# Mixture-of-experts block: eight slots of 32 tokens in four 32-column tiles, a new order of slots, and alternating heads in the scan's products

## The chip, the cores and the metric

The kernel runs on one core of a Trainium2 chip. The metric is the device time of one execution in microseconds (us), from the core's first to its last instruction with what the launch adds. The core's engines are called as in the profile: PE (TensorE, with PEld for its weight loads), DVE (VectorE), ACT (ScalarE), POOL (GpSimd) and SP (the queue from which most loads are issued).

## What is computed

Two blocks follow each other on 512 tokens of width 1024. The first mixes a bidirectional state-space scan (32 heads of 64, 4 groups, chunks of 128 tokens) with a Fourier branch, and then sends each token through 4 of 32 experts. The second has attention, a gated recurrence and a dense feed-forward part. The change touches the scan and the experts of the first block:

```python
# scan, per chunk (forward, and backward on the reversed sequence); the two directions are added
cb = jnp.einsum('bclgn,bcsgn->bcgls', cc, bc)
y_diag = jnp.einsum('bcgls,bcghls,bcsghp->bclghp', cb, decay_in, xdt)
y_off = jnp.einsum('bclgn,bcghpn,bclgh->bclghp', cc, h_prev, jnp.exp(a_cs))

# experts: 512 tokens x 4 choices = 2048 rows over 32 experts
logits = (tok @ w_router + b_router).astype(jnp.float32)
top_logit, top_idx = lax.top_k(logits, TOP_K)
top_w = jax.nn.softmax(top_logit, axis=-1)
gu = xe @ w_gate_up[e] + b_gate_up[e]              # 1024 -> 2048, for the rows of expert e
gate = jnp.minimum(gu[:, :D_FF], SWIGLU_LIMIT)
up = jnp.clip(gu[:, D_FF:], -SWIGLU_LIMIT, SWIGLU_LIMIT)
act = (up + 1.0) * gate * jax.nn.sigmoid(SWIGLU_ALPHA * gate)
y = act @ w_down[e] + b_down[e]                    # 1024 -> 1024, times the row's weight, added to its token
```

All weights are float32. One expert's are 8 MB (up) and 4 MB (down), so 32 experts read 384 MB.

## The kernel before

**The scan.** `mixer` walks over 16 pairs of heads (`p`). For each pair PE projects the next pair's inputs (`px`, `pc`, three reduced-precision products for one of float32, lines 99 to 101), builds the states (`pst`), and then does the diagonal part `py` (line 669) and the part from the states `po` (line 677). `py` is one PSUM bank of 128 partitions: head `j` = 0 takes partitions 0 to 63, head 1 takes 64 to 127, and four token blocks `b` and two directions `d` are accumulated into each. The loops run over `j`, then `d`, then `b`, so that four products in a row, and then four more, go to the same half of the partitions. These products are full float32; in the trace one of them is two PE instructions.

**The experts.** `moe` handles 32 slots in the order of `ORDER`. Slots 0 and 1 are experts 0 and 1, so that their weights can be loaded before the router has finished; the other slots hold the other experts by the number of their tokens, the smallest first. A slot has a width, which is the number of tokens that it has room for:

- slots 0 to 15 (`HALF`) are half slots, of 64 tokens. The 64 tokens are the stationary operand of a 128x64 product, and two such products, with different columns of the weights, run into the lower and the upper 64 partitions of PSUM (`half_mm`, line 1262). These are float32 products straight from the loaded weights (`wraw`).
- slots 16 to 29 are full slots, of 128 tokens. Here the weights are split by ACT (`whi`, line 86) and DVE (`wlo`, line 87) into two reduced-precision parts, and three products (lines 99 to 101) do the work of one.
- slots 30 and 31 (`DOUBLE`) are a full and a half block with the same weights.

Experts with more tokens than their slot has room for get further passes of a loop at the end (`For_i`), as often as the router's counts need; on these inputs the loop runs zero times.

In turn `t` PE does the up products of slot `t` (tile `pgh` of a half slot, `pg` of a full one) and the down products of the slot before (`pd`, or `pdh` beside a full block). Tokens are gathered by an indirect DMA (`h_scr` to `xg`), transposed on PE (`pt`), and the result is scaled on ACT, multiplied by `g2b` on POOL (line 1336) and added to its rows in DRAM by an indirect DMA (`x_scr`). Half slots gather and scatter half rows of 2 KB.

Weights come in pieces of 1 MB, eight for up and four for down of each slot, all issued from SP in the order of use, into a ring of 13 buffers (`W.rings`). A piece is loaded as soon as the buffer 13 pieces earlier has been used up. The instruction order on each engine is fixed at build time by a scheduler.

The lines that pick the width and the order are:

```python
HALF = range(0, 16)
DOUBLE = (30, 31)
ORDER = (0, 1, 16, 17, 2, 3, 18, 19, 4, 20, 5, 21, 6, 30, 7, 8, 22, 9, 23, 10, 24, 11, 31, 12, 13, 25, 26, 14, 27, 28,
         29, 15)
```

Of the kernel before, what the change touches and what calls it, by code (L numbers as in the profile page):

```python
# [8 lines left out]
F32 = mybir.dt.float32  # L9
F32R = mybir.dt.float32r  # L10
BF16 = mybir.dt.bfloat16
I32 = mybir.dt.int32
# [6 lines left out]
P = 128  # L19
D = 1024  # L20
# [84 lines left out]
TILE_WAITS = ('moeio', 'moeio3', 'ps_g', 'ps_mt', 'ps_d', 'outr', 'outp', 'mx', 'biasp', 'rows', 'b2io', 'b2t', 'b2r', 'res2', 'moeT', 'wraw3', 'wraw4')  # L105


class Kernel:
# [91 lines left out]
    def mixer(self):  # L200
# [391 lines left out]
        for p in range(16):  # L592
# [22 lines left out]
            for j in range(2):  # L615
                for d in range(2):
# [269 lines left out]
    def router(self, mx, keep, xT, ahead, st, stp):  # L886
# [59 lines left out]
        def choose(b, x1, rs, fill=lambda: None):  # L946
# [23 lines left out]
            self.chosen = nc.vector.tensor_scalar(pick[:, b, :], iota[:, 0:64], r[:, 0:1], None, op0=ALU.is_equal).ins  # L970

        def picked(b):

            for k in range(KD):
                nc.tensor.matmul(pts[0][:, k % 4, 64 * (k // 4):64 * (k // 4) + 64], h2s[b][0][:, k * P:(k + 1) * P],
# [13 lines left out]
        pick = xT[:, 0:256].rearrange("p (b l) -> p b l", l=64)  # L989
# [17 lines left out]
        xT4 = xT[:, 512:].rearrange("p (k t) -> p k t", k=4)  # L1007
        nc.scalar.copy(xT4[:, 0:2, :], pts[0][:, 0:2, :])
        nc.vector.tensor_copy(xT4[:, 2:4, :], pts[0][:, 2:4, :])
        ahead()  # L1010

        with self.behind((self.chosen,)):
            p0 = psl.tile([P, 1, 3], F32, tag='ptab', name='ptab0')
            self.table(rot, p0[:, 0, :], rm[:, :, 1:2], V[:, :, 1, 0:3], True, True)
            first = self.slots(keep, p0, 1, 'f', (0,))[0]
# [53 lines left out]
    def table(self, pool, out, place, v, first, half=False):  # L1069
# [3 lines left out]
        v4 = lambda x: x.rearrange("p b (h l) -> p b h l", h=2)  # L1073
        if half:
            nc.vector.tensor_tensor(v4(pe), self.rc[:, 0, None, None, 0:64].to_broadcast([P, NT, 2, 64]),
                                    place[:, :, :, None].to_broadcast([P, NT, 2, 64]), op=ALU.is_equal)
# [16 lines left out]
    def overflow(self, tp, psl, selb, ubf, obf, keep):  # L1093
# [3 lines left out]
        nc, cf = self.nc, self.rc  # L1097
# [10 lines left out]
        val = tp.tile([P, 2, 16], BF16, name='val')  # L1108
        for i, c in enumerate((16, 40)):
            nc.vector.tensor_scalar(val[:, i, :], cf[:, 2, 24:40], pos, cf[:, 2, c:c + 1], op0=ALU.is_equal, op1=ALU.mult)  # L1110
        nc.tensor.matmul(pc[:, 8:40], obf, val.rearrange("p i q -> p (i q)"), start=True, stop=True,
                         skip_group_check=True)
        nc.tensor.matmul(pc[:, 40:41], obf, fl, start=True, stop=True, skip_group_check=True)
        self.ext = ext = keep.tile([P, 33], F32, name='ext')
        nc.vector.tensor_copy(ext, pc[:, 8:41])

        no = tp.tile([P, 16], F32, name='noblk')
        nc.vector.tensor_scalar(no, ext[:, 16:32], 0.0, 4096.0, op0=ALU.is_equal, op1=ALU.mult)
        nc.vector.tensor_add(ext[:, 16:32], ext[:, 16:32], no)
        self.exti = keep.tile([P, 33], I32, name='exti')  # L1120
# [23 lines left out]
    def slots(self, pool, tab, n, sfx, halves=()):  # L1144


        nc = self.nc
        t = pool.tile([P, n, tab.shape[2]], F32, name='slott' + sfx)
# [6 lines left out]
        for j in halves:  # L1155
            nc.vector.tensor_scalar(f[:, 0, j:j + 1], f[:, 0, j:j + 1], 2.0, self.rc[:, 2, 41:42], op0=ALU.mult, op1=ALU.add)
# [7 lines left out]
    HALF = range(0, 16)  # L1164
# [830 lines left out]
```

## Time and profile before

| what | value |
|---|---|
| time, median of 3 runs | 2924.7 us (2928.36, 2915.26, 2924.7) |
| time of the profiled execution | 2918.13 us |
| its span, first to last instruction | 2916.3 us |
| PE busy | 2772.1 us, 95% |
| mean granted TensorE clock | 0.984 |
| DMA, mean over the span | 221 GB/s |
| scan of the first block | about 130 to 800 us |
| experts | about 950 to 2080 us |

Busy time of PE counts an instruction from its start to a modelled end, so neighbouring instructions overlap, and the step from one start to the next is the better price of one. A DMA share is the mean busy share of the core's 16 DMA engines; it can come out a little above 1. The profiled execution is 6.6 us faster than the median.

### The profile page before, as it was taken

How to read it: one execution, taken by the hardware profiler on the slowest of the kernel's cores; microseconds unless marked ns; L12 is line 12 of the kernel's file. 1: busy time of each engine (PE TensorE's matmuls, PEld its weight loads, DVE VectorE, ACT ScalarE, POOL GpSimd, SP SyncE). 2: the span in 40 equal slices, each digit the busy share in tenths (PEclk: the TensorE clock that was granted, in tenths of full speed). 3: DMA queues.
4: the chain of work that ended last, by engine and by line, in shares of the span. 5: the costliest groups of instructions: out<-in, count | busy, mean ns of one | idle time of the engine just before them, and what ended most of it. 6: DMA issues, size and time to landing. Idle time of an engine off the chain costs nothing. (4 is left out here: it accounts for less than half of the span.)

```text
span 2916.3 us, 37264 instructions
## 1 busy us (share of the span) xinstructions
PE 2772.1 (95%) x14084; PEld 2033.2 (70%) x14084; DVE 1773.7 (61%) x2557; ACT 1321.1 (45%) x1899; POOL 403.5 (14%) x388
## 2 busy tenths in 40 slices
PE   5999999999999999999999999999599999999999
PEld 3888878788887455555455554657288888788887
DVE  4637878787677565766445552768477777733322
ACT  4534545454444244544334442556356666632221
POOL 1211121212202111111111112120300000100000
PEclk9999999999999899999999999999799999999999
DMA  8243374744566899999699979998532132533321
GB/s 229 80 137 96 113 220 134 228 126 138 179 188 246 343 387 401 359 391 400 258 402 408 389 293 386 399 382 342 147 101 83 55 87 73 188 97 91 101 94 65
DMA packets 294839, 644.40 MB, mean 221 GB/s; under 512 B 18706, under 2 KB 190370, under 8 KB 258848
## 3 DMA queue, kind: packets, MB, share of 16 engines
q1 hardware_dynamic: 267552, 569.77, 53.3%
q0 software_dynamic: 25120, 67.93, 8.6%
q10 hardware_dynamic: 1984, 4.28, 0.4%
q8 instruction: 112, 1.84, 0.3%
q14 instruction: 71, 0.58, 0.1%
HBM read 617.54 MB, written 33.64 MB: 223 GB/s over the span
## 5 line engine op out<-in xcount | busy, mean ns | idle before, releaser
L87 DVE TENSOR_TENSOR wlo<-wraw,whi 128x1024 fp32r<-128x1024 f32 (+1 forms) x635 | 787.8, 1264 | 462.1 <-ACT whi L86 451.5
L86 ACT CAST whi<-wraw 128x1024 fp32r<-128x1024 f32 (+1 forms) x635 | 652.5, 1043 | 605.5 <-PE pf L100 153.2
L1262 PE MATMUL pgh<-wraw,xg 128*64 128x512 f32 x1152 | 279.7, 605 | 0.7 <-ACT xg L1241 0.7
L99 PE MATMUL px<-hThi,whi 128*128 128x512 f32 x576 | 229.9, 400 | 0.0
L101 PE MATMUL px<-hThi,wlo 128*128 128x512 f32 x576 | 225.9, 392 | 2.1 <-DVE wlo L87 2.1
L100 PE MATMUL px<-hTlo,whi 128*128 128x512 f32 x576 | 226.4, 393 | 0.0
L1262 PEld LDWEIGHTS pgh<-wraw,xg 128*64 128x64 f32 x1152 | 81.8, 138 | 154.0 <-issue 147.6
L1336 POOL TENSOR_TENSOR y<-y,g2b 64x512 f32<-64x512 f32 (+1 forms) x50 | 86.1, 1723 | 522.2 <-ACT y L1331 497.4
L100 PE MATMUL pg<-wlo,T0h 128*128 128x512 f32 x352 | 144.2, 410 | 5.5 <-DVE wlo L87 5.4
L100 PE MATMUL pf<-hnlo,whi 128*128 128x512 f32 (+1 forms) x384 | 142.4, 372 | 0.0
L101 PE MATMUL pf<-hnhi,wlo 128*128 128x512 f32 (+1 forms) x384 | 142.4, 372 | 0.0
L99 PE MATMUL pf<-hnhi,whi 128*128 128x512 f32 (+1 forms) x384 | 141.6, 372 | 0.0
L101 PE MATMUL pg<-whi,T0l 128*128 128x512 f32 x352 | 140.4, 399 | 0.0
L99 PE MATMUL pg<-whi,T0h 128*128 128x512 f32 x352 | 132.4, 405 | 3.4 <-ACT whi L86 3.4
L484 DVE SCALAR_TENSOR_TENSOR cacc<-cr,vecs,cacc 128x770 f32<-128x770 f32 (+1 forms) x128 | 121.7, 961 | 19.8 <-ACT cacc L482 18.7
L101 PEld LDWEIGHTS px<-hThi,wlo 128*128 128x128 f32 x576 | 108.3, 188 | 27.6 <-DVE wlo L87 2.9
L1262 PE MATMUL pd<-wraw,act 128*64 128x512 f32 x512 | 122.7, 599 | 0.0
L100 PEld LDWEIGHTS px<-hTlo,whi 128*128 128x128 f32 x576 | 109.0, 189 | 16.0 <-issue 1.7
L99 PEld LDWEIGHTS px<-hThi,whi 128*128 128x128 f32 x576 | 109.0, 189 | 15.7 <-issue 1.7
L1267 DVE TENSOR_SCALAR g<-pgh 128x512 f32<-128x512 f32 x18 | 12.4, 691 | 170.4 <-PE pgh L1262 170.3
L1268 ACT ACTIVATE g<-g 128x512 f32<-128x512 f32 (+1 forms) x34 | 28.2, 831 | 178.9 <-DVE g L1267 178.9
L623 ACT ACTIVATE m<-m,acs_tok 128x128 f32<-128x128 f32 x256 | 81.6, 390 | 58.3 <-DMA m<-acs_scr 56.6
(614 smaller groups left out, 6102.3 us busy)
## 6 DMA issues: line engine op xcount, KB each, us to landing
wraw<-in_w_gate_up SPq DMA_DIRECT2D x256, 1024.0 KB, 9.7
wraw<-in_w_down SPq DMA_DIRECT2D x128, 1024.0 KB, 9.9
wraw<-in_w_in SPq DMA_DIRECT2D x81, 512.0 KB, 6.6
wraw<-in_w_mod SPq DMA_DIRECT2D x23, 1024.0 KB, 9.1
wraw<-in_w_ffn_in SPq DMA_DIRECT2D x44, 512.0 KB, 5.2
wraw<-in_w_in SPq DMA_DIRECT2D x18, 1024.0 KB, 5.4
m<-acs_scr POOLq DMA_DIRECT2D x64, 256.0 KB, 5.3
wraw<-in_w_ffn_out SPq DMA_DIRECT2D x10, 1024.0 KB, 5.0
```

Source lines behind the costliest of these rows:

```text
L86: a = (copy or nc.scalar.copy)(dst[0], src)
L87: return a.ins, (eng or nc.vector).tensor_sub(dst[1], src, dst[0].bitcast(F32)).ins
L99: nc.tensor.matmul(out, a[0], b[0], start=first, stop=False)
L100: nc.tensor.matmul(out, a[0], b[1], start=False, stop=False)
L101: return nc.tensor.matmul(out, a[1], b[0], start=False, stop=last).ins
L484: nc.vector.scalar_tensor_tensor(acc, t[:, j:j + n], cw[:, j, ch:ch + 1], acc, op0=ALU.mult, op1=ALU.add)
L623: nc.scalar.activation(m[:, b, :], m[:, b, :], AF.Relu, bias=acs_tok[:, b, row:row + 1], scale=-1.0)
L1262: nc.tensor.matmul(out[64 * h:64 * h + 64], a, w, start=False, stop=last, skip_group_check=True)
L1267: nc.vector.tensor_scalar_min(g, gate, 7.0)
L1268: nc.scalar.activation(g, g, AF.Silu, scale=1.702)
L1336: nc.gpsimd.tensor_mul(y[q], y[q], g2b[q, c])
```

## The change

Three edits are made together.

1. **Quarter slots.** Slots 0 to 7 get a width of 32 tokens. Four products of 128x32, each with another part of the weights' columns, go to the four 32-partition parts of PSUM (`part_mm`). The tokens of such a slot are gathered and scattered as quarter rows of 1 KB. An up piece is still four products of 512 columns; a down piece is now eight products of 256 columns where a half slot has four of 512. `HALF` and `DOUBLE` become the table `WIDTHS`, the helpers take a width in place of a flag, the limits for the closing loop follow the widths, and that loop can hold 24 passes in place of 16.
2. **A new `ORDER`** of the slots.
3. **The scan's `py` products** run over `d`, then `b`, then `j`: consecutive products go to the two heads in turn. The tables `m` are made in the order of that use.

Besides, the pool of four rows of 1024 (`moeio3`) becomes three of these, and four rows of 512 (`moeio4`, tile `low`) for half and quarter slots.

```diff
-            for j in range(2):
-                for d in range(2):
+            for d in range(2):
+                for j in range(2):
                     row = 32 * d + h0 + j
                     m = pr4.tile([P, NT, P], F32, tag='m', name='m')
...
-            for j in range(2):
-                for d in range(2):
-                    for b in range(NT):
-                        nc.tensor.matmul(py[j * HD:(j + 1) * HD, b, :], xd[d][:, b, j, :], ms[2 * j + d][:, b, :],
+            for d in range(2):
+                for b in range(NT):
+                    for j in range(2):
+                        nc.tensor.matmul(py[j * HD:(j + 1) * HD, b, :], xd[d][:, b, j, :], ms[2 * d + j][:, b, :],
...
-    HALF = range(0, 16)
-    DOUBLE = (30, 31)
-    ORDER = (0, 1, 16, 17, 2, 3, 18, 19, 4, 20, 5, 21, 6, 30, 7, 8, 22, 9, 23, 10, 24, 11, 31, 12, 13, 25, 26, 14, 27, 28,
-             29, 15)
+    WIDTHS = ((8, (32,)), (16, (64,)), (30, (128,)), (32, (128, 64)))
+    ORDER = (0, 1, 16, 17, 8, 18, 9, 10, 19, 30, 2, 11, 20, 12, 21, 13, 22, 14, 3, 23, 24, 25, 4, 26, 27, 28, 5,
+             15, 29, 31, 6, 7)
+
+    NX = 24
...
-        io3 = self.pool('moeio3', 4, None, st)
+        io3 = self.pool('moeio3', 3, None, st)
+        io4 = self.pool('moeio4', 4, None, st)
...
-            nc.gpsimd.indirect_dma_start(out=x[:, :D // 2] if half else x, out_offset=None,
-                                         in_=halfrows(self.h2_d) if half else self.h2_d,
+            nc.gpsimd.indirect_dma_start(out=x[:, :D * w // P], out_offset=None, in_=rows(self.h2_d, w),
                                          in_offset=bass.IndirectOffsetOnAxis(ap=tok, axis=0),
...
-        def half_mm(out, xT, k, ws, last):
-            a = xT[:, k % 4, 64 * (k // 4):64 * (k // 4) + 64]
-            for h, w in enumerate(ws):
-                nc.tensor.matmul(out[64 * h:64 * h + 64], a, w, start=False, stop=last, skip_group_check=True)
+        def columns(w, x):
+
+            n = P // w
+            v = x.rearrange("p (g q c) -> p g q c", q=n, c=D // n)
+            return [v[:, :, q, :] for q in range(n)]
...
+        def part_mm(w, out, xT, k, ws, last):
+
+            n = KD * w // P
+            a = xT[:, k % n, k // n * w:k // n * w + w]
+            for i, o in enumerate(out):
+                for q, wq in enumerate(columns(w, ws)):
+                    m = wq.shape[1] // len(out)
+                    nc.tensor.matmul(o[w * q:w * q + w], a, wq[:, m * i:m * i + m, :], start=False, stop=last,
+                                     skip_group_check=True)
...
-                for q, c in qs:
+                for i in range(P // w):
+                    q, c = slice(w * i, w * i + w), slice(n * i, n * i + n)
                     if tail:
                         nc.vector.scalar_tensor_tensor(y[q], pd[q], wgt[q], g2b[q, c], op0=ALU.mult, op1=ALU.mult)
                     else:
                         nc.gpsimd.tensor_mul(y[q], y[q], g2b[q, c])
```

The scheduler decides where the new products stand, so three places of PE's order are shown. First the scan, one pair of heads. The numbers behind `m` and `xd` are buffers: `m_1920` and `m_1928` belong before to the two directions of head 0, and after to the two heads of the forward direction. Before:

```order
L101 MATMUL px_2048<-hThi_82,wlo_1899 128x512
L669 MATMUL py_2076<-m_1920,xd_1902 64x128 x4
L669 MATMUL py_2076<-m_1928,xd_1903 64x128 x4
L669 MATMUL py_2076<-m_1936,xd_1902 64x128 x4
L669 MATMUL py_2076<-m_1944,xd_1903 64x128 x4
L677 MATMUL po_2093<-C0_1785,Hn_2028 128x128
L677 MATMUL po_2093<-C0_1785,Hn_2033 128x128
```

After, the middle of the 16 products, where the direction changes:

```order
L669 MATMUL py_2076<-m_1920,xd_1902 64x128
L669 MATMUL py_2076<-m_1928,xd_1902 64x128
L669 MATMUL py_2076<-m_1920,xd_1902 64x128
L669 MATMUL py_2076<-m_1928,xd_1902 64x128
L669 MATMUL py_2076<-m_1936,xd_1903 64x128
L669 MATMUL py_2076<-m_1944,xd_1903 64x128
L669 MATMUL py_2076<-m_1936,xd_1903 64x128
L669 MATMUL py_2076<-m_1944,xd_1903 64x128
L669 MATMUL py_2076<-m_1936,xd_1903 64x128
```

Sixteen products are sixteen products; four in a row with one table become pairs that change the table, and with it the half of the partitions, at each step.

Second, the start of the experts, slot 0 (`xg_7499` are its tokens, `sel` and `bh` its bias, `pperm` and `povf` the end of the router). Before:

```order
L1254 LDWEIGHTS sel_7532
L1254 MATMUL pgh<-bh,sel_7532 64x512
L1254 LDWEIGHTS sel_7532
L1254 MATMUL pgh<-bh,sel_7532 64x512
L1262 MATMUL pgh<-wraw,xg_7499 64x512 x11
L1038 LDWEIGHTS eb
L1038 MATMUL pperm<-esel,eb 1x32
L1262 MATMUL pgh<-wraw,xg_7499 64x512 x2
L1101 LDWEIGHTS selb
```

After:

```order
L1277 LDWEIGHTS sel_7532
L1277 MATMUL pgh<-bh,sel_7532 32x512
L1277 LDWEIGHTS sel_7532
L1277 MATMUL pgh<-bh,sel_7532 32x512
L1288 MATMUL pgh<-wraw,xg_7499 32x512 x15
L1041 LDWEIGHTS eb
L1041 MATMUL pperm<-esel,eb 1x32
L1288 MATMUL pgh<-wraw,xg_7499 32x512 x3
L1105 LDWEIGHTS selb
```

The products keep their number and their 512 columns, and write 32 partitions in place of 64; the router's last products stand between them at a slightly later place.

Third, the turn behind double slot 30: the down products of the slot before it (`pd`), between the first up products of the slot behind it (`pgh`). Before, slot 6 (half) stands ahead and slot 7 (half) behind:

```order
L1262 MATMUL pd_11530<-wraw_11533,act_11048 64x512 x4
L1262 MATMUL pd_11530<-wraw_11539,act_11048 64x512 x4
L1262 MATMUL pd_11530<-wraw_11551,act_11048 64x512 x4
L1262 MATMUL pd_11530<-wraw_11557,act_11048 64x512 x4
L1262 MATMUL pgh_11584<-wraw_11623,xg1_7500 64x512 x4
L1262 MATMUL pgh_11584<-wraw_11629,xg1_7500 64x512 x4
L1262 MATMUL pgh_11584<-wraw_11635,xg1_7500 64x512 x4
```

After, slot 19 (full) stands ahead and slot 2 (quarter) behind:

```order
L1288 MATMUL pgh_10644<-wraw_10661,xg1_7500 32x512 x4
L1288 MATMUL pgh_10644<-wraw_10684,xg1_7500 32x512 x4
L1252 MATMUL pt_10702<-ident_66,row_10264 128x128 x8
L1272 LDWEIGHTS esel_8111
L1272 MATMUL pd_10528<-bh_6817,esel_8111 128x512
L1272 LDWEIGHTS esel_8111
L1272 MATMUL pd_10528<-bh_6817,esel_8111 128x512
L99 MATMUL pd_10528<-whi_10533,T0h_8231 128x512
L100 MATMUL pd_10528<-wlo_10534,T0h_8231 128x512
L101 MATMUL pd_10528<-whi_10533,T0l_8232 128x512
```

What is done in the double's wake is now a quarter's up and a full slot's down, where it was a half's up and a half's down.

## Rows read from the trace of the kernel before

**Rows 1.** the page, its head and busy times by engine (share of the span, instructions)
```profile
span 2916.3 us, 37264 instructions
...
PE 2772.1 (95%) x14084; PEld 2033.2 (70%) x14084; DVE 1773.7 (61%) x2557; ACT 1321.1 (45%) x1899; POOL 403.5 (14%) x388
```

**Rows 2.** windows: length, busy us of PE, PEld, DVE, ACT, POOL; clock, DMA share, GB/s
```profile
930.00:2050.00 1120.00, 1072.76 (x4845) 615.92 (x4846) 649.96 (x758) 492.75 (x517) 187.19 (x117) 0.98 0.95 370
1450.00:1690.00 240.00, 227.44 (x1007) 124.43 (x1006) 120.65 (x113) 99.55 (x107) 46.03 (x30) 0.99 1.01 400
1110.00:1370.00 260.00, 244.43 (x1137) 144.07 (x1134) 159.51 (x203) 118.86 (x124) 49.56 (x30) 0.99 0.99 388
130.00:760.00 630.00, 627.25 (x3755) 533.92 (x3754) 455.42 (x762) 303.65 (x608) 115.06 (x197) 1.00 0.48 144
```

**Rows 3.** windows of 40 us in the experts' stage, same columns
```profile
1370.00:1410.00 40.00, 40.00 (x162) 23.21 (x163) 26.43 (x31) 20.28 (x21) 4.62 (x2) 0.96 0.75 283
1410.00:1450.00 40.00, 40.00 (x183) 16.91 (x179) 12.94 (x12) 9.03 (x10) 4.11 (x3) 1.00 0.69 259
...
1690.00:1730.00 40.00, 40.00 (x159) 22.97 (x158) 23.01 (x19) 20.56 (x21) 6.32 (x3) 1.00 0.83 312
1730.00:1770.00 40.00, 40.00 (x180) 16.46 (x180) 11.46 (x11) 8.57 (x12) 2.54 (x2) 1.00 0.69 270
...
1970.00:2010.00 40.00, 37.57 (x164) 28.53 (x163) 34.97 (x30) 28.86 (x30) 5.00 (x2) 1.00 0.87 335
```

**Rows 4.** timeline of the SP queue: start, length of the group, loads
```profile
1469.69 18.37 SPq L61 DMA_DIRECT2D wraw<-in_w_gate_up  x8
...
1696.64 41.38 SPq L61 DMA_DIRECT2D wraw<-in_w_gate_up  x8
```

**Rows 5.** groups by line: count, busy us, mean ns, idle before
```profile
L1262 PE MATMUL pgh<-wraw,xg 128*64 128x512 f32 x1152 | 279.7, 605 | 0.7 <-ACT xg L1241 0.7
...
L1262 PE MATMUL pd<-wraw,act 128*64 128x512 f32 x512 | 122.7, 599 | 0.0
...
L1254 PE MATMUL pg<-bh,esel 96*128 96x512 bf16 x64 | 19.3, 383 | 9.7 <-DVE act L1269 9.7
...
L1245 PE MATMUL pt<-ident,act 128*128 128x128 f32 x128 | 17.4, 278 | 1.7 <-DVE act L1270 0.9 <-DVE slott L1149 0.8
L1245 PE MATMUL pt<-ident,xg 128*128 128x128 f32 x128 | 17.4, 277 | 1.5 <-DVE T1l L93 1.5
...
L515 PE MATMUL pm<-wraw,sc 128*32 128x512 f32 x128 | 16.2, 601 | 0.3 <-DMA wraw<-in_w_mod 0.3
```

**Rows 6.** timeline of PE inside a full slot: start, us, instruction
```profile
1049.90 0.40 PE L100 MATMUL pg<-wlo,T1h 128*128 128x512 f32 x1
...
1051.54 0.39 PE L100 MATMUL pg<-wlo,T1h 128*128 128x512 f32 x1
```

**Rows 7.** windows of 5 us at the start of the experts' stage
```profile
950.00:955.00 5.00, 3.98 (x18) 1.97 (x19) 5.00 (x19) 0.37 (x1) 0.00 (x0) 0.50 0.54 221
955.00:960.00 5.00, 5.00 (x21) 1.73 (x19) 1.50 (x4) 0.00 (x0) 1.11 (x1) 0.86 0.55 187
```

**Rows 8.** windows of 5 us at the end of the experts' stage
```profile
2055.00:2060.00 5.00, 3.68 (x17) 2.88 (x18) 4.75 (x5) 5.00 (x6) 0.00 (x0) 1.00 0.31 100
...
2075.00:2080.00 5.00, 1.96 (x10) 0.50 (x6) 1.50 (x2) 0.00 (x0) 0.87 (x1) 0.94 0.81 183
```

**Rows 9.** DMA queues from 955 to 963 us: packets, MB, share
```profile
q0 software_dynamic: 80, 0.09, 3.4%
```

**Rows 10.** groups by line: the scan's products
```profile
L669 PE MATMUL py<-m,xd 128*64 128x128 f32 x512 | 53.7, 276 | 0.0
```

**Rows 11.** timeline of PE in the scan, one pair of heads
```profile
258.99 3.33 PE L669 MATMUL py<-m,xd 128*64 128x128 f32 x32
262.25 2.05 PE L677 MATMUL po<-C,Hn 128*128 128x128 f32 x16
```

**Rows 12.** timeline of PE in the router
```profile
937.71 1.98 PE L975 MATMUL pt<-xg,h 128*128 128x64 f32 x16
```

More of the change, by code (lines that the diff above doesn't have):

```diff
@@ L1067, in router, with table @@
         return first
-    def table(self, pool, out, place, v, first, half=False):
+    def table(self, pool, out, place, v, first, w=P):
         nc = self.nc
         pe = pool.tile([P, NT, P], BF16, tag='pe', name='pe')
[L1073 to L1076, printed above, removed]
+        n = P // w
+        if n > 1:
+            nc.vector.tensor_tensor(pe.rearrange("p b (h l) -> p b h l", h=n),
+                                    self.rc[:, 0, None, None, 0:w].to_broadcast([P, NT, n, w]),
+                                    place[:, :, :, None].to_broadcast([P, NT, n, w]), op=ALU.is_equal)
         else:
@@ L1142, in extra, with slots @@
         return r[:, 0, :, None], v
-    def slots(self, pool, tab, n, sfx, halves=()):
-        nc = self.nc
-        t = pool.tile([P, n, tab.shape[2]], F32, name='slott' + sfx)
+    def slots(self, pool, tab, sfx, widths, tmp=None):
+        nc, n = self.nc, len(widths)
+        t = (tmp or pool).tile([P, n, tab.shape[2]], F32, name='slott' + ('' if tmp else sfx))
         nc.vector.tensor_copy(t, tab)
@@ new lines, in bias @@
+        def bias(w, out, selT, c, n):
+            b = bh[:, c:c + D * n]
+            if w == P:
+                for i, o in enumerate(out):
+                    nc.tensor.matmul(o, selT.to_broadcast([96, P]), b[:, 512 * i:512 * i + 512], start=True, stop=False)
+                return
+            for q, bq in enumerate(columns(w, b)):
+                for i, o in enumerate(out):
+                    g = n // len(out)
+                    nc.tensor.matmul(o[w * q:w * q + w], selT.to_broadcast([96, w]), bq[:, g * i:g * i + g, :],
+                                     start=True, stop=False, skip_group_check=True)
@@ L1359, in moe @@
         for s_ in self.ORDER:
-            blocks += [(s_, 0, s_ in self.HALF)] + ([(s_, P, True)] if s_ in self.DOUBLE else [])
+            ws = self.widths(s_)
+            blocks += [(s_, sum(ws[:i]), w) for i, w in enumerate(ws)]
         at = lambda e: [i for i, b in enumerate(blocks) if b[0] == e]
@@ L1369, in step @@
                 if j < n:
-                    e, o, half = blocks[i0 + j]
+                    e, o, w = blocks[i0 + j]
                     src = self.rm[:, :, e:e + 1]
@@ L1389, in moe @@
             nx = at(self.ORDER[turn + 1]) if turn < NE - 1 else []
+            assert not (nx and len(xTs) == 2 and xTs[0][0] < P and blocks[nx[0]][2] == P)
             if e < 2:
@@ L1951, in layout @@
     rc[:, 0, :] = l
[L1952 removed]
+    rc[:, 2, 41], rc[:, 2, 42] = l // 64, l // 32
     rc[:, 1, :] = l[:, None] < l
```

185 lines of the change are left out of this document (94 added, 91 removed).

## The prediction

> **What bounds the kernel now.** I began with the page's busy times [rows 1]: TensorE (PE) is busy for 2772.1 of 2916.3 us, so work taken off it can shorten the run, but only where no other engine ends last. That is asked stage by stage, with the windows view [rows 2]. In the scan's stage (130 to 760 us) PE is busy for 627.25 of 630 us and the DMA engines for 48%: PE alone is the bound, and a microsecond saved there is a microsecond of the run. In the experts' stage (930 to 2050 us) two things are nearly full at once: PE 1072.76 of 1120 us, DMA share 0.95. So 0.05 x 1120 = 56 us is all that the loads could still give there, however little PE has to do.
>
> Where do the loads pause? The 40 us windows [rows 3] show it: shares of 0.75 and 0.69 from 1370 us, 0.83 and 0.69 from 1690 us, which is 22.4 and 19.2 us of idle DMA, while PE stands at 40.00. These are the places of the two double slots (30 and 31): PE falls behind, the 13 pieces of buffer fill, the loads wait. A smaller one is at 1970 us (0.87, 5.2 us), in the run of full slots at the end. The SP queue's timeline gives the pace of the loads in between [rows 4]: seven slots from 1469.69 to 1696.64 us, 32.4 us a slot.
>
> **What a slot costs PE.** Half slot: two alternating column halves take 279.7 / 1152 = 0.243 us an instruction of 512 columns (one float32 product is two) [rows 5]. 18 half blocks have 64 such up and 32 down (122.7 / 512 = 0.240): 15.5 + 7.7 = 23.2, with about 2 us of biases and transposes 25. Full slot: 144 products at the step seen from 1049.90 to 1051.54 us, seven products later [rows 6], 0.234 us: 33.7; transposes and biases (17.4 + 17.4 + 19.3) / 16 = 3.4 [rows 5]; together 37. Double: 62. A quarter slot is not in the trace, but four 32-column tiles with four different streams are: `pm` at L515, 16.2 / 128 = 0.127 us an instruction [rows 5]. Up is again 64 of 512 columns, 8.1 us; down is 64 of 256 columns, between half of that (4.1) and the same (8.1), I take 5. With half the transposes, 14.5. So each of eight slots loses about 10.5 us, 84 us of PE in all (bounds 60 and 95).
>
> **What of the 84 us shows.** Against 32.4 us of loads, a full slot puts PE 4.6 us behind, a double 30, a half lets it gain 7.4, a quarter 18; it can't get ahead of the loads, so the lag stops at zero. Before, both doubles begin at a lag near 0 and reach 30; the pauses of 22 and 19 say that the ring covers about 10. In the new order each double stands behind a full slot (19, 30 and 29, 31): 35 at its end, 25 us of pause by this count. But behind it now comes a quarter, which empties the ring at about 1 us a piece (8 x 0.127) where a half takes 1.9 (8 x 0.243), and part of the pause lies in that following slot (the windows at 1410 and 1730 us). I take 0 for the doubles, bounds -10 and +10. The runs of three full slots (23 to 25, 26 to 28) reach 14, 4 over the cover, twice; that answers to the 5.2 at the end before: 0, bounds -8 and +4. The rest of the idle 56 us is thin (0.99 from 1110 us [rows 2]): -3.
>
> The start: from 950 to 960 us the share is 0.54 and 0.55 [rows 7], 4.5 us of pause, because slot 0's pieces hold the ring while PE works on them at half pace. Quarters free them in half the time: -4 (0 to -5).
>
> The end: the last weights land at about 2056.5 us (share 0.31 of 5 us from 2055), and PE ends at 2077 (1.96 us busy from 2075) [rows 8]: 20 us, in which slot 29's and 15's down products are caught up. With slots 6 and 7 last, PE gains 18 on each and is left with a down piece of 1 to 2 us and the closing chain, so I take -15 (-8 to -18). The first weights of the next block that are loaded in this shadow still lie beside the last scatter.
>
> Gathers and scatters: the first eight slots hold 178 tokens (counted by the reference's own router on its inputs: 25, 23, 16, 17, 18, 24, 25, 30). Rows of 1 KB instead of 2 make 356 more packets each way. In 955 to 963 us slot 1's gather is 80 packets, 0.09 MB, 3.4% of 8 us on 16 engines, 4.4 us of engine time for 46 rows [rows 9], 0.095 each: at that price 712 more cost 4.2 us of all 16 engines, at no price nothing; +2. POOL's two multiplications become four half as long, on an engine that is busy for 14% [rows 1]: nothing, and if they showed it would be behind the last slot only, whose product is DVE's. Smaller swiglu, tables and copies on DVE and ACT lie beside the loads. A second ring of four low rows and three full rows takes the place of four: a full slot's result waits for a scatter one slot old, which is some 30 us; nothing.
>
> Experts' stage: 0 + 0 - 3 - 4 - 15 + 2 = -20 (the bounds add up to -44 and +10).
>
> **The scan's products.** `py`: 512 instructions, 53.7 us [rows 10]; 32 a pair of heads, from 258.99 us to the next product at 262.25, 0.102 each [rows 11]. Four in a row went to one column half; now the halves alternate. Nearest row: the alternating halves of L1262, 0.243 for 512 columns, where one half at a time at py's rate would be 4 x 0.102 = 0.41; the same ratio makes 53.7 into 32, -22. But the streams are four times shorter, and weights may set the pace: with 128 weight columns and only 64 streamed, L975 goes no faster than (1.98 - 0.28) / 15 = 0.113 [rows 12], so 64 weight columns about 0.057, 512 x 0.057 = 29, -25. Adding L1262's excess over a plain halving (0.243 - 0.204 = 0.04 an instruction) to 0.051 gives 0.09, 46.6, -7. I take -18; bounds 0 and -26 (a perfect halving). PE has nothing else to wait for in this stage, so it passes to the run whole.
> A rule of the Trainium skill speaks against it: TensorE: Matmul & The Clock Gate, "Part 3: Packing small matmuls — row/col tiling", says that a weight load runs beside a product in flight only where the two differ in their row group, and here both heads use all 128 rows. By that rule py gains nothing, and the sum is -20 instead of -38. The trace leans the other way: L1262's two halves share all rows as well and run at 0.243, not 0.41.
>
> **Sum.** -20 - 18 = -38 on the profiled execution's 2918.1 us: 2880. That execution lies 6.6 us below the median of 2924.7 and 3.5 below the mean of the four times; 2880 + 3 gives **2883 us**. A measurement of this kernel tells about 0.5% (15 us) from no change.
>
> **Rivals.**
> *Only the scan gains.* If the count of lags holds (25 us at each double, 4 at each run of three) the +18 eat the end's -15 and the start: 2921.6 - 18 = 2904. For it: the loads are at 1.01 wherever PE isn't behind [rows 2]; against: the quarter right behind each double.
> *Only the experts' stage gains*: the weights of one head's half are not loaded before the other's stream is through, and py takes its 53.7 us as now [rows 10]: 2921.6 - 20 = 2902. For it: py has 128-column streams, a quarter of those of L1262 behind which a load can hide.
> *The loads never pause again*: all 56 us and the end's share beyond it, 2921.6 - 18 - 60 = 2844. For it: 414 MB (370 GB/s x 1120 us) at 400 GB/s is 1036 us [rows 2]; against: a double still needs twice its loads' time.
> *Both small*: PE's order or the row loads eat them, 2912 to 2925.
> *Slower.* One count above 32 in the first eight slots brings a pass of the closing loop: a slot's loads that nothing hides (32 us), and most of a full slot's 37 behind them, some 60: 2883 + 60 = 2943; it decides from the 33rd token on. The nearest is 30, and the 46 rows in slot 1's gather are the 23 tokens that I counted, so it should not happen.
>
> **How the numbers follow.** The forecast (2868 to 2895) 0.50; only the scan (2895 to 2911) 0.15; only the experts 0.12; no more pauses (2838 to 2868) 0.13; both small 0.06; slower 0.04. Faster by over 0.5% (below 2910): 0.50 + 0.12 + 0.10 + 0.13 = 0.85, less 0.02 for what I don't see, 0.83; within 0.5%: 0.13; slower 0.04. For 8 in 10 I leave out the far end of the third rival and what lies above 2911: 2846 to 2911.
>
> **What would show it.** py near 30 to 40 us by lines, at unchanged instruction count, and the scan's stage shorter by as much. Up products of quarter slots at 0.11 to 0.13 us. PE idle in the experts' stage growing from 47 us [rows 2] to over 100, DMA share 0.95 or a little more, pauses still behind the doubles. Last weights to PE's end below 8 us. Wrong if the quarter's four tiles run one after another (0.24 or more an instruction), if the granted clock, 0.98 over the stage now, falls so far in quarter slots that the next full slot starts late (at the lower level a quarter would take 29 us, still under 32.4), or if the doubles' pauses grow to 30.

## The result

The changed kernel takes 2829.35 us (median of 4 runs, 2828.14 to 2830.84) against 2924.43 us: a ratio of 0.9679, 95% interval 0.9656 to 0.9703. That is 95 us less. The forecast was 2883 us with a range of 2846 to 2911: the direction was right, the size less than half of what came. The profiled execution has 2828.8 us.

The head of the page after (lines as in [rows 1]):

```profile
span 2827.0 us, 37725 instructions
...
PE 2665.5 (94%) x14326; PEld 1992.1 (70%) x14326; DVE 1766.2 (62%) x2559; ACT 1315.5 (47%) x1899; POOL 416.4 (15%) x402
```

TensorE lost 106.6 us of work (2772.1 to 2665.5), the span 89.3. To see where, both spans are cut at the same four events. The first is the experts' fifth load: four of their 384 pieces are issued 53 us earlier in both kernels (from 869.97 and 855.97 us), and the steady stream of the other 380 begins with the fifth. In the SP queue's timeline (start, length, loads) of the kernel before, these are the group with the fifth load and the one with the last.

```profile
923.27 37.91 SPq L61 DMA_DIRECT2D wraw<-in_w_gate_up  x12
...
2021.14 24.24 SPq L1348 DMA_DIRECT2D wraw<-in_w_down  x8
```

The same two groups of the changed kernel:

```profile
909.24 36.51 SPq L61 DMA_DIRECT2D wraw<-in_w_gate_up  x12
...
1941.48 25.00 SPq L1378 DMA_DIRECT2D wraw<-in_w_down  x8
```

The last issue is the end of the second group, 2045.4 and 1966.5. When the last weights land in the changed kernel is seen in PE's timeline, where the last 16 products of the experts wait for them (in brackets: idle before, and what ended it):

```profile
1975.82 2.77 PE L1288 MATMUL pd<-wraw,low 128*32 128x256 f32 x48
1980.35 1.07 PE L1288 MATMUL pd<-wraw,low 128*32 128x256 f32 x16 [1.75 <-DMA wraw<-in_w_down]
```

And POOL's timeline from there to the second block's first work (L86):

```profile
1982.63 1.59 POOL L1367 DMA_INDIRECT x_scr<-row,sloti  x1 [0.28 <-POOL low L1366]
1990.64 1.56 POOL L1367 DMA_INDIRECT x_scr<-low,sloti  x1 [6.42 <-DMA x_scr<-row,sloti]
1994.56 1.55 POOL L1367 DMA_INDIRECT x_scr<-low,sloti  x1 [2.36 <-DMA x_scr<-low,sloti]
1999.02 1.55 POOL L1367 DMA_INDIRECT x_scr<-low,sloti  x1 [2.91 <-DMA x_scr<-low,sloti]
2003.89 5.58 POOL L86 CAST whi<-wraw 128x1024 fp32r<-128x1024 f32 x4 [3.32 <-issue]
```

In the kernel before, the last weights land at about 2056.5 and PE ends at 2077.0 [rows 8]; POOL's timeline has its last scatter and that L86 at

```profile
2086.80 1.56 POOL L1337 DMA_INDIRECT x_scr<-y,sloti  x1 [6.09 <-DMA x_scr<-y,sloti]
2093.14 5.58 POOL L86 CAST whi<-wraw 128x1024 fp32r<-128x1024 f32 x4 [4.78 <-issue]
```

So:

| stretch | before | after | difference | forecast |
|---|---|---|---|---|
| span's start to the fifth load of experts | 923.3 | 909.2 | -14.0 | -18 |
| fifth load issued to last weights landed | 1133.2 | 1071.1 | -62.1 | -5 |
| last weights landed to PE's last product | 20.5 | 1.1 | -19.4 | -15 |
| PE's last product to the second block | 16.1 | 22.5 | +6.4 | 0 |
| second block | 823.2 | 823.1 | -0.1 | 0 |

The forecast's -5 is 0 for the doubles, 0 for the runs of full slots, -3 thin, -4 at the start, +2 for the rows. Nearly everything that was missed lies in this one line: the loads pause far less than forecast.

The windows of the whole experts' stage show the same from PE's side (length; busy us of PE, PEld, DVE, ACT, POOL; clock, DMA share, GB/s). Before:

```profile
923.00:2077.00 1154.00, 1099.10 (x4952) 631.69 (x4952) 668.21 (x788) 505.45 (x535) 191.13 (x120) 0.98 0.93 363
```

After:

```profile
909.00:1981.00 1072.00, 1006.63 (x5190) 609.52 (x5194) 662.83 (x787) 501.05 (x535) 200.20 (x130) 0.97 0.99 390
```

PE is rid of 92.5 us and the stage of 82. PE's idle time grows by 10 only, from 55 to 65. Before, PE was busy for 95% of the stage and the DMA engines for 0.93; now PE is at 94% and the DMA engines at 0.99.

The groups by line (count, busy us, mean ns of one, idle before), answering to [rows 5] and [rows 10]:

```profile
L1288 PE MATMUL pgh<-wraw,xg 128*64 128x512 f32 x640 | 149.3, 597 | 0.0
...
L1288 PE MATMUL pgh<-wraw,xg 128*32 128x512 f32 x512 | 71.1, 642 | 0.5 <-ACT xg L1255 0.5
...
L1288 PE MATMUL pd<-wraw,low 128*32 128x256 f32 x512 | 34.3, 393 | 1.7 <-DMA wraw<-in_w_down 1.7
...
L669 PE MATMUL py<-m,xd 128*64 128x128 f32 x512 | 31.5, 276 | 0.0
```

An up product of a quarter takes 71.1 / 512 = 0.139 us, a down product 34.3 / 512 = 0.067, so a slot's 64 and 64 take 8.9 + 4.3 = 13.2 (forecast 8.1 + 5). `py` falls from 53.7 to 31.5.

Last, the 40 us windows in which loads still pause, answering to [rows 3]:

```profile
1210.00:1250.00 40.00, 40.00 (x159) 21.36 (x156) 24.96 (x21) 19.91 (x20) 4.51 (x2) 1.00 0.77 291
1250.00:1290.00 40.00, 38.15 (x209) 19.13 (x208) 24.01 (x40) 17.13 (x20) 6.35 (x4) 1.00 0.87 338
...
1890.00:1930.00 40.00, 38.66 (x177) 20.79 (x175) 24.58 (x22) 18.61 (x19) 1.58 (x1) 1.00 0.86 325
```

Slot 30 now costs 0.23 x 40 + 0.13 x 40 = 14.4 us of idle DMA where it cost 22.4, slot 31 costs 5.6 where it cost 19.2.

### The profile page after: what moved, and what is told of

It is laid out like the page before. It is cut to its first block, busy times and chain, and to the rows that moved or that the text cites. A ratio compares the mean times of both kernels' runs of the same rounds, so it can differ in the third digit from the quotient of the medians.

```text
span 2827.0 us, 37725 instructions
## 1 busy us (share of the span) xinstructions
PE 2665.5 (94%) x14326; PEld 1992.1 (70%) x14326; DVE 1766.2 (62%) x2559; ACT 1315.5 (47%) x1899; POOL 416.4 (15%) x402
## 5 line engine op out<-in xcount | busy, mean ns | idle before, releaser
L86 ACT CAST whi<-wraw 128x1024 fp32r<-128x1024 f32 (+1 forms) x635 | 654.8, 1045 | 583.2 <-PE pf L100 157.3
L1288 PE MATMUL pgh<-wraw,xg 128*64 128x512 f32 (+1 forms) x1152 | 220.4, 617 | 0.5 <-ACT xg L1255 0.5
L1288 PEld LDWEIGHTS pgh<-wraw,xg 128*64 128x64 f32 (+1 forms) x1152 | 59.5, 127 | 117.9 <-issue 108.2
L100 PE MATMUL pg<-wlo,T0h 128*128 128x512 f32 x288 | 118.1, 410 | 4.3 <-DVE wlo L87 4.2
L1294 DVE TENSOR_SCALAR g<-pgh 128x512 f32<-128x512 f32 (+1 forms) x18 | 10.3, 572 | 178.3 <-PE pgh L1288 178.3
L99 PEld LDWEIGHTS px<-hThi,whi 128*128 128x128 f32 x576 | 109.8, 191 | 16.4 <-issue 1.7
L100 PEld LDWEIGHTS px<-hTlo,whi 128*128 128x128 f32 x576 | 109.8, 191 | 14.4
L101 PE MATMUL pg<-whi,T0l 128*128 128x512 f32 x288 | 115.9, 403 | 0.1
L1295 ACT ACTIVATE g<-g 128x1024 f32<-128x1024 f32 (+2 forms) x34 | 26.6, 782 | 185.6 <-DVE g L1294 185.6
L99 PE MATMUL pg<-whi,T0h 128*128 128x512 f32 x288 | 106.4, 403 | 4.0 <-ACT whi L86 4.0
L99 PE MATMUL px<-h2hi,whi 128*128 128x512 f32 x256 | 104.0, 406 | 0.0
L100 PE MATMUL px<-h2lo,whi 128*128 128x512 f32 x256 | 102.8, 402 | 0.0
```

What stands on the lines that cost most here:

```text
L86: a = (copy or nc.scalar.copy)(dst[0], src)
L99: nc.tensor.matmul(out, a[0], b[0], start=first, stop=False)
L100: nc.tensor.matmul(out, a[0], b[1], start=False, stop=False)
L101: return nc.tensor.matmul(out, a[1], b[0], start=False, stop=last).ins
L1288: nc.tensor.matmul(o[w * q:w * q + w], a, wq[:, m * i:m * i + m, :], start=False, stop=last, skip_group_check=True)
L1294: nc.vector.tensor_scalar_min(g, gate, 7.0)
```

## The experiments

Here is what the loads did in each kernel. The window is from the experts' fifth issue ("first" from here on) to the last, 380 pieces of 1024 KB (1.05 MB, as a MB is 10^6 bytes in these views). Idle is the sum of 5 x (1 - DMA share) over windows of 5 us from the first issue to 10 us after the last, shares over 1 taken as 1. The packets' time per MB is the share of the weights' queue (q1) times the window's length, by its MB, up to 6 us after the last issue. Landing is the median from issue to landing of a gate/up load (the first profile of the changed kernel has none; it is taken from its second). Window, idle, packets and landing are of one profiled execution each. The changed kernel's second has 1055.9, 31.2 and 2.470.

| kernel | us | window | idle | us per MB | landing |
|---|---|---|---|---|---|
| before | 2924.4 | 1122.1 | 76.5 | 2.505 | 9.7 |
| scan alone | 2912.5 | 1129.4 | 76.9 | 2.514 | 9.0 |
| scan, order (halves) | 2881.0 | 1108.3 | 61.6 | 2.503 | 11.2 |
| scan, widths (old order) | 2851.9 | 1078.4 | 45.8 | 2.477 | 16.6 |
| widths, order (old scan) | 2841.6 | 1059.5 | 33.0 | 2.472 | 16.4 |
| changed kernel | 2829.4 | 1057.2 | 32.8 | 2.470 | 16.9 |
| the same, 11 buffers | 2840.3 | 1075.5 | 47.6 | 2.476 | 15.8 |
| doubles between quarters | 2823.9 | 1047.4 | 29.2 | 2.468 | 15.3 |
| the same, half ahead | 2832.6 | 1062.6 | 32.6 | 2.486 | 11.8 |
| all halves | 2773.0 | 1008.3 | 10.1 | 2.444 | 20.7 |
| all quarters | 2748.7 | 985.9 | 5.2 | 2.445 | 20.5 |
| all quarters, 8 buffers | 2762.9 | 998.9 | 18.6 | 2.444 | 18.8 |
| all quarters, 5 buffers | 2768.8 | 1008.9 | 19.7 | 2.449 | 11.3 |

The kernel before, timed beside them in three groups, had 2919.2, 2919.6 and 2921.2 us.

The weights' queue over the window and 6 us more (q1: packets, MB, share of 16 engines), before and in the changed kernel:

```profile
q1 hardware_dynamic: 71136, 398.61, 88.5%
...
q1 hardware_dynamic: 70783, 397.30, 92.3%
```

0.885 x 1128.1 / 398.61 = 2.505 and 0.923 x 1063.2 / 397.30 = 2.470.

### The three edits apart

**The scan alone.** The kernel before with this:

```diff
-            for j in range(2):
-                for d in range(2):
-                    for b in range(NT):
+            for d in range(2):
+                for b in range(NT):
+                    for j in range(2):
```

> The kernel before with the scan's alternation alone; the experts' stage is the old one. In the changed kernel the 512 products of py take 31.5 us instead of 53.7, but the experts' first weights are issued only 14.0 us earlier (909.24 instead of 923.27). Theory 'handed on': the stage's gain reaches the end of the run as it is, about -14 us, 2910; py 31 to 32 us. Theory 'swallowed': the experts' loads set the end anyway, and an earlier start only makes a longer pause: 0 to -5, above 2919. Theory 'the alternation costs nothing and gains all': -22, 2902.

Measured: 2912.47 us, ratio 0.9976 (0.9965 to 0.9987), -6.8 us beside 2919.23. Between the first two theories: of -14, about half. The first load is issued 13.6 us earlier (909.7), but the loads' window is 7.3 us longer at the same idle time (76.9).

**The scan left out.** The changed kernel with the old loops.

> The changed kernel with the scan's products in the old order (one head after the other, 128 products each). All theories that let the stage's gain through give the changed kernel's 2829 + 14 = 2843. 'Swallowed' gives 2829 to 2834. py 53 to 54 us again.

Measured: 2841.61 us, ratio 0.9731 (0.9710 to 0.9751): 12.3 us above the changed kernel, 13.7 above its second timing (2827.95). Here the -14 is handed on. So the scan's gain reached the end in full ahead of the new experts' stage, and about half of it ahead of the old one. Why half was lost there was not settled: the window that is 7 us longer is of one execution, and those of the kernel before in the same group lie between 2914.6 and 2925.3 us.

**The widths alone.** The changed kernel with the old `ORDER`.

> The changed kernel with the old order of slots: the first eight slots are quarters, but both doubles stand where they stood and the last slots are 28, 29, 15 (full, full, half). The changed kernel's loads, first issue to last, take 1057 us where before took 1122: -65. Theory 'width': quarter slots keep TensorE ahead of the loads wherever they stand: nearly all of the -65 stays, and only the end (-10 net) goes back: about 2840. Theory 'order': the width gives only what lies in the thin pauses, 10 to 20 us: 2880 to 2890. Theory 'both are needed': slots 2 to 7 now stand in the first half of the stage, before slot 30, where TensorE was not far behind; they cure 30 and not 31 nor the end: -14 for the scan and about -30 for the loads, 2875 to 2885, with the pause at slot 31 as before (about 20 us).

Measured: 2851.87 us, ratio 0.9765 (0.9744 to 0.9785). Nearest to "width", but no theory has it. Its windows at slot 30 (first two) and 31:

```profile
1350.00:1390.00 40.00, 40.00 (x242) 18.81 (x240) 14.84 (x14) 10.65 (x12) 2.88 (x4) 1.00 0.83 312
1390.00:1430.00 40.00, 39.12 (x178) 15.98 (x176) 11.83 (x19) 10.42 (x12) 10.17 (x7) 1.00 1.03 403
1650.00:1690.00 40.00, 40.00 (x151) 19.24 (x149) 16.28 (x15) 10.90 (x12) 1.56 (x1) 1.00 0.61 226
1690.00:1730.00 40.00, 40.00 (x172) 16.48 (x168) 13.19 (x14) 11.32 (x14) 5.16 (x4) 1.00 0.91 362
```

Slot 30 now stands between two quarters (6, 30, 7) and pauses for 0.17 x 40 = 6.8 us instead of 22.4. Slot 31, between halves as before, keeps 0.39 x 40 + 0.09 x 40 = 19.2. The quarters' effect is local: all eight are used up before slot 31 and do nothing for it.

**The order alone.** The changed kernel with `WIDTHS = ((16, (64,)), (30, (128,)), (32, (128, 64)))`.

> The changed kernel with half slots in place of the quarters (widths as before) and the new order of slots. Theory 'width': no more than the scan's gain, 2905 to 2912, with pauses of 20 us at both doubles. Theory 'order': the doubles' new places and the two light slots at the end give most of the gain: 2850 to 2870. Theory 'both are needed': order alone about 0 in the loads, since the run of 26, 27, 28 and the doubles still put TensorE behind and half slots win back only 7 us each; the end gains 0 to 10: 2900 to 2912.

Measured: 2880.97 us, ratio 0.9866 (0.9843 to 0.9889). None of the three has it: the order alone gives more than "width" and "both are needed" allow and less than "order". From the kernel with the scan alone, the order takes 31.5 us, the widths 60.6, both together 83.1: nearly a sum. In the loads' window it is 21, 51 and 72. The pauses by 5 us windows are 17 us at slot 30 and 14 at slot 31, where they were 22.8 and 19.3 before, and 14.8 and 6.0 in the changed kernel.

### How far the loads can go

**All quarters, 13 buffers.** `WIDTHS = ((32, (32,)),)`, and the limits of the closing loop raised so that it stays empty.

> The changed kernel with all 32 slots as quarters: each slot computes 32 tokens and the tokens beyond them are left out (the closing pass too). TensorE then needs 15 us a slot against 32 of loads, so that no load ever waits for a buffer. So far the loads' window (first to last issue) is 1122 us before, 1129 with the scan alone, 1108 with the order, 1078 with the widths and 1057 with both; of that the idle share of the DMA engines is 77, 77, 62, 46, 33 us, and what is left is 1046, 1052, 1047, 1033, 1024. Theory 'pauses alone': the rest is the loads' own time and its spread is chance: about 1030 to 1045 here, idle below 8. Theory 'queue': with more loads waiting in the queue, as now (16 us from issue to landing instead of 9), each MB itself takes less time: window 1015 to 1025, packets' time 2.46 to 2.47 us a MB against 2.507 before and 2.472 in the changed kernel.

Measured: window 985.9 us, below every value expected, idle 5.2, all of it at the start. Part of the fall is the rows that are not moved (q0's packets: 9.5 MB and 37.7 us instead of 17.4 MB and 63.8). "Pauses alone" falls: 2.445 us a MB, not 2.505. "Queue" does not reach these values either.

**All quarters, 8 buffers.**

```diff
-        W.rings = [w2] * 4 + [w3] * 2 + ring + [w2] + [w3] * 2 + [w4]
+        W.rings = [w2] * 4 + ring + [w2]
```

> As the last one (32 quarters, tokens left out), with 8 buffers of weights in the ring instead of 13. Theory 'pauses alone' (or: half-width products slow the transfers): TensorE is far ahead, 8 MB in flight or waiting are enough; as with 13, 2.46 to 2.48 us a MB. Theory 'queue': the fewer loads stand in the queue the longer each MB takes: 2.50 or more, and the window 10 to 20 us longer than with 13 buffers.

Measured: 2.444 us a MB. It tells nothing against the queue, since the landing of 18.8 us shows that 18.8 / 2.6 = 7 loads still stood in it; the longer window is an idle start (18.0 us in the first 35).

**All halves.** `WIDTHS = ((32, (64,)),)`, with the same limits.

> The changed kernel with all 32 slots as halves of 64 tokens (tokens beyond them left out), 13 buffers. TensorE needs 25 us a slot against 32: no pauses either, but each piece stands in its buffer nearly twice as long as with quarters. Theory 'pauses alone': window as with all quarters within 5 us. Theory 'queue': between all quarters and the kernel before: 2.48 to 2.50 us a MB, loads landing 13 to 20 us after issue. Theory 'half-width products slow the transfers': 2.51 us a MB as in the kernel before, window 1035 or more with no idle share.

Measured: window 1008.3 us, 2.444 us a MB. Products of half width do not slow transfers.

**All quarters, 5 buffers.** `W.rings = [w2]`.

> 32 quarters (tokens beyond 32 a slot left out) with 5 buffers in the ring. With 13 and with 8 buffers the loads took 2.444 us a MB and landed 20.5 and 18.8 us after issue, so that 7 loads stood in the queue in both and the last test told nothing of the queue. With 5 buffers at most 4 loads can stand there, 9 to 11 us from issue to landing, as in the kernel before. Theory 'queue': 2.49 to 2.52 us a MB as there, loads' window 1005 to 1020. Theory 'full slots': it is the work of full slots (their splits read and write the same memory while loads land) that lengthens the packets' time, not the depth of the queue: 2.44 to 2.46 us a MB, window 990 to 1000 plus what the idle share shows.

Measured: 2.449 us a MB with landing after 11.3 us. The view of DMA queues from 980 to 1900 us (q1: packets, MB, share of 16 engines):

```profile
q1 hardware_dynamic: 65971, 370.82, 98.5%
...
wraw<-in_w_gate_up SPq DMA_DIRECT2D x237, 1024.0 KB, 11.4
```

"Queue" falls: four loads in the queue are as good as seven. "Full slots" is not shown either, as the traces tell. In the kernel before, the first q1 row is of 1383 to 1438 us (in slot 30's pause), the second of 1470 to 1690 us (no pause):

```profile
q1 hardware_dynamic: 1850, 11.05, 55.1%
...
wraw<-in_w_gate_up SPq DMA_DIRECT2D x8, 1024.0 KB, 4.8
...
q1 hardware_dynamic: 14791, 83.67, 94.0%
```

and in the changed kernel from 980 to 1200 us (no pause):

```profile
q1 hardware_dynamic: 15518, 86.91, 96.5%
```

In the pause a MB takes 0.551 x 55 / 11.05 = 2.74 us; without pauses 0.940 x 220 / 83.67 = 2.47 in the one and 0.965 x 220 / 86.91 = 2.44 in the other, both with full slots among theirs. Cutting the whole stage of both kernels into 10 us windows: where the DMA share is 1.005 or more, a MB takes 2.45 us in both (64 windows before, 82 after). Where it is less, it takes 2.6 us on the mean: 48 windows with 147 MB before, 23 windows with 75 MB after. Against the 2.444 us of the runs without pauses these windows hold about 23 us of longer packets before, and about 9 after. So the stretched time goes with the pauses: while loads are let in one by one, each takes longer, and the idle share shows only part of what is lost.

### Places of the doubles, and the ring

**Doubles between quarters.** The changed kernel with

```diff
-    ORDER = (0, 1, 16, 17, 8, 18, 9, 10, 19, 30, 2, 11, 20, 12, 21, 13, 22, 14, 3, 23, 24, 25, 4, 26, 27, 28, 5,
-             15, 29, 31, 6, 7)
+    ORDER = (0, 1, 16, 17, 18, 2, 30, 3, 19, 20, 8, 4, 31, 5, 21, 9, 22, 10, 23, 24, 11, 12, 25, 13, 26, 14, 15, 27,
+             28, 29, 6, 7)
```

> The changed kernel with another order of slots: each double stands between two quarters (2, 30, 3 and 4, 31, 5) in the first half of the stage, and 28, 29, 6, 7 end it. In the run with the old order slot 30 stood between two quarters and its pause was 7.1 us, against 14.8 in the changed kernel (quarter behind it only) and 22.8 before (halves on both sides); slot 31 between halves kept 19.4. Theory 'neighbours': 7 us of pause at each double and 5 at the start, none elsewhere; the last scatters are two instead of four behind the last product: 2829 - 8 - 5 = 2816, at best 2810. Theory 'moved': what the middle loses by the missing quarters comes back as pauses in the runs of full slots: 2825 to 2835.

Measured: 2823.93 us, ratio 0.9672 (0.9659 to 0.9686). Windows at slot 30 and slot 31:

```profile
1120.00:1170.00 50.00, 48.62 (x277) 23.78 (x277) 21.02 (x27) 14.05 (x15) 5.33 (x6) 1.00 0.71 256
1340.00:1370.00 30.00, 28.71 (x202) 15.45 (x204) 14.62 (x22) 8.89 (x11) 3.20 (x4) 1.00 0.80 297
```

The time is between the two theories. 0.29 x 50 = 14.5 us at slot 30, 0.20 x 30 = 6 at slot 31. Three scatters still stand behind the last product (from 1980.1, 1988.3 and 1992.8 us). The neighbours are the same; what differs is ahead of them: three full slots (16 to 18) before 2, 30, 3, and a half (8) before 4, 31, 5.

**A half ahead.** `ORDER = (0, 1, 16, 17, 8, 2, 30, 3, 18, 19, 9, 4, 31, 5, 20, 21, 10, 22, 23, 24, 11, 12, 25, 13, 26, 14, 27, 28, 15, 29, 6, 7)`.

> As the order with each double between two quarters, but with a half slot ahead of the first quarter (8, 2, 30, 3 instead of 18, 2, 30, 3 after a run of three full slots), and 28, 15, 29, 6, 7 at the end instead of 28, 29, 6, 7. There the pause was 14.3 us at slot 30, behind three full slots, and 5.9 at slot 31, which had a half ahead of its quarter. Theory 'lag ahead of the double': both pauses now 5 to 7 us, -8, and the four scatters at the end stand less close, 0 to -5: 2812 to 2818. Theory 'place in the stage' (the first double pauses more because it comes early): 14 us again, 2822 to 2828.

Measured: 2832.60 us, ratio 0.9697 (0.9683 to 0.9710), and the same two places:

```profile
1130.00:1160.00 30.00, 28.14 (x218) 13.80 (x217) 12.56 (x21) 7.10 (x9) 5.82 (x7) 1.00 0.85 335
1330.00:1370.00 40.00, 37.84 (x253) 18.09 (x252) 17.73 (x26) 10.72 (x15) 6.27 (x7) 1.00 0.79 301
```

Slot 30's pause falls to 0.15 x 30 = 4.5: the lag ahead of a double sets its pause, not its place in the stage. But the kernel is slower than the order before, by 8.7 us where 8 less were expected. Slot 31 now has 8.4, and between 615 and 700 us after the first issue, around the full slots 22 to 24, 7.7 us came where the order before had 1.5; a MB takes 2.486 us. The slack was moved, not made.

**11 buffers.** The changed kernel with

```diff
-        w3, w4 = (self.pool(f'wraw{i}', n, None, st, 'right') for i, n in ((3, 4), (4, 1)))
-        W.rings = [w2] * 4 + [w3] * 2 + ring + [w2] + [w3] * 2 + [w4]
+        w3, w4 = (self.pool(f'wraw{i}', n, None, st, 'right') for i, n in ((3, 2), (4, 1)))
+        W.rings = [w2] * 4 + [w3] * 2 + ring + [w2] + [w4]
```

> The changed kernel with 11 buffers of weights in the ring instead of 13; 2.6 us of loads a buffer. Its pauses now are 14.8 us at slot 30, 6 at slot 31, 5 at the start. Theory 'cover': a pause is the lag of TensorE less what the ring covers, so two buffers less add 5 us at each double and up to 5 where the lag was just covered (three full slots in a row, twice): pauses together 45 to 60 instead of 33, total 2845 to 2860. Theory 'the double's pause is only its split work' (weights released by the splits, not by the ring): no change above 3 us, 2829 to 2833.

Measured: 2840.27 us, ratio 0.9721 (0.9704 to 0.9737), idle 47.6 instead of 32.8: 19.0 at slot 30 (+4.2), 13.4 at slot 31 (+7.4), 8.4 at the start (+3.4). So a double's pause is not only its split work: the ring covers the lag, 2 to 4 us a buffer. The time is 5 us below the range of "cover", and the runs of three full slots added nothing.

**The changed kernel again**, timed beside the last order and the shorter ring:

> The changed kernel itself, so that the other orders are compared with it on one chip: 2829 if nothing but the order differs between the calls; no theory hangs on it.

Measured: 2827.95 us, ratio 0.9689 (0.9672 to 0.9706). Both orders with the doubles between quarters have intervals that overlap this one: none of the versions tried is shown to be faster than the changed kernel.

## Why the prediction was wrong

**The step that failed** is "What of the 84 us shows", the step that says how much of PE's freed time the loads give back. It put the loads at -5 us, and -62 came. Two parts of it were wrong: the terms of what the pauses lose, and the ceiling over them.

*The terms.* The doubles stood at 0, the runs of full slots at 0, the thin pauses at -3: the loads were to be held up nearly as often as before. Idle time fell by 43.7 us all the same. For packets that take less time the forecast had no term: 398 MB at 0.035 us less a MB are -14. Together these make -58 of the -62.

*The ceiling.* "0.05 x 1120 = 56 us is all that the loads could still give there, however little PE has to do". The -5 did not need it, but the rival "the loads never pause again" was priced by it, and the range ends near that rival. Three things were wrong with it.

- The forecast's own rows contradict it. 414 MB at 400 GB/s are 1036 us of the 1120, which leaves 84. And seven slots took 32.4 us each [rows 4]: the 380 pieces of the window are 31.7 slots, 1027 us at that pace, where 1122.1 were taken. The loads lost some 95 us there, not 56.
- The window 930 to 2050 us leaves out the end. Over the whole stretch of loads idle time is 76.5 us.
- A share of busy DMA engines does not see the packets stretched in and around the pauses: about 23 us before, 9 after. The 32.4 us a slot was not a floor either: all halves take 1008.3 / 31.7 = 31.8, in part because they move fewer rows.

**Term by term.** The freed PE work was right: 84 us forecast (60 to 95), 92.5 measured. What shows of it was not. *Doubles*: 0 (-10 to +10), measured (14.8 - 22.8) + (6.0 - 19.3) = -21 us of idle time by the 5 us windows. The forecast charged each double for the full slot ahead of it and let the quarter right behind it win back just that. About half of the -21 came with the order alone, where half slots stand in the quarters' places (17 and 14), the rest with the quarters. How much a pause shrinks hangs on the slots ahead as well: with quarters on both sides it was 6.8 and 4.5 us at slot 30, but 14.5 where three full slots stand ahead of the first quarter. *Start*: -4; measured -5.2 (10.2 to 5.0). *Runs of three full slots, thin idle*: 0 and -3; measured -43.7 + 21.3 + 5.2 = -17. That quarters keep the lag small between the doubles too is the likely reason, but it was not tested by itself. *Packets*: no term; -14. *Rows*: +2; q0's packets took 66.6 us before and 63.8 after, so nothing. *End*: -15 (-8 to -18); measured -19.4, then +6.4 given back, because four scatters, each behind the landing of the one before, stand between the last product and the second block, where two stood before. From the last product to the second block it is 16.1 us with two, 20.1 with three (doubles between quarters) and 22.5 with four. The forecast had no term for them; that the net -13 lies near its -15 is luck.

**The scan**: -18 (0 to -26). `py` fell by 22.2, as the ratio of the nearest row had it, and the first load came 14.0 us earlier. The -18 was a middle between that ratio and two other counts. Of the difference of 8.2, from the first to the last `py`, PE's waits rose by 2.0 us (2.3 instead of 0.3) and the busy time of its other products by 5.2. Most of that is `pm`, 16.2 us before [rows 5]; why was not traced:

```profile
L515 PE MATMUL pm<-wraw,sc 128*32 128x512 f32 x128 | 20.4, 602 | 1.0 <-DMA wraw<-in_w_mod 1.0
```

One pair of heads in PE's timeline, answering to [rows 11]:

```profile
260.10 1.97 PE L669 MATMUL py<-m,xd 128*64 128x128 f32 x32
262.00 2.05 PE L677 MATMUL po<-C,Hn 128*128 128x128 f32 x16
```

32 products step through in 1.90 us, 0.059 each, where they took 3.26. What happens is seen in windows of 50 ns of the `py` products alone (length, busy us and number of PE, PEld, DVE), first before, then after:

```profile
260.00:260.05 0.05, 0.05 (x3) 0.05 (x2) 0.00 (x0) 1.00 0.00 0
...
261.00:261.05 0.05, 0.05 (x6) 0.05 (x4) 0.00 (x0) 1.00 0.00 0
```

Three products were under way at a time, and now there are six. In the single records of the trace one product lasts 273 ns in both kernels. Before, one starts every 109 ns; after, two start 7 ns apart, one for each head, and the next two 109 ns later. So the two heads' products run side by side.

The rule weighed in the forecast (the Trainium skill, TensorE: Matmul & The Clock Gate, "Part 3: Packing small matmuls — row/col tiling") lets a weight load hide only behind a product of another row group. The forecast took from it that `py` would stay at 53.7. That did not follow: the 22.2 us are gone though both heads use all 128 rows, and they came from products side by side, not from a hidden load. This trace does not agree with the rule itself either. The weight loads are recorded beside products of the same rows, before the change too, and a `py` product of 128 columns every 109 ns and a pair of L1262 with 512 every 429 ns (records of the kernel before) leave 2 ns for anything that does not grow with the columns.

**The rivals.** "The loads never pause again", 2844, is the one on the right side. Its time is too high by the same ceiling: loads still pause in the changed kernel (32.8 us idle), and it is at 2829 all the same. "Only the scan" counts +18 by lags; its own terms make 2 x 25 + 2 x 4 less the 41.6 of before, +16. "Only the scan", "only the experts" and "both small" fall by the two tests that part the edits. "Slower" did not come up: no pass of the closing loop is in the trace.

**The signs.** `py` at 30 to 40 us: yes. Up products at 0.11 to 0.13 us: 0.139 by busy time, which counts the tail of each group of eight. Last weights to PE's end below 8 us: 1.1. PE idle "to over 100": no. Over the stage it is 65, because the stage shrank with PE's work; that sign was drawn from a stage that keeps its length.

## What to carry to other kernels

Where two resources are both above 90% and take turns at ending last, a reduction of one can come through almost whole: read the room not from the busy share alone but from the undisturbed pace times the number of pieces against the time really taken. Here that was some 95 us where the share said 56, and it was in the rows; the change got 65 of it (window 1122.1 to 1057.2). A block that takes twice its loads' time wants cheap blocks behind it and no lag ahead of it; moving cheap blocks there takes them from elsewhere, so a better pause at one place is not yet a faster kernel.

## What the runs showed of the hardware

**Loads let in one by one cost more than their idle time.** 2.74 us of packets' time a MB in the pause of slot 30, 2.45 with a stream that never stops, be it four or seven loads deep. What in the transfer takes longer then was not shown.

**Quarter slots do not hold the clock when they wait for loads.** With all quarters (windows as above):

```profile
930.00:1900.00 970.00, 633.85 (x4581) 146.33 (x4585) 92.09 (x320) 53.52 (x128) 167.22 (x181) 0.73 1.02 410
1400.00:1440.00 40.00, 23.98 (x192) 5.60 (x192) 1.18 (x3) 2.13 (x5) 9.42 (x12) 0.79 1.02 412
```

PE is busy for 634 of 970 us, with a gap ahead of nearly every piece, and the granted clock, 1.00 in windows with full slots, is 0.73 on the mean, between the levels of 1.2 and 2.4 GHz; the timeline there has groups of eight up products of 1.06 us, of 1.94 us and some between. It costs no time there: 1.94 is still under the 2.5 us between two loads. In the changed kernel, with full slots between the quarters, the clock over the stage is 0.97.
